# Storing two rows each of batches 10 and 11, instead of two rows of batch 11, so that one DMA engine is left out

## The chip, the cores and the metric

One NeuronCore of a Trainium2 chip runs the kernel. The metric is the device time of one execution in microseconds. Before the change it is 125.07 us, the median of 16 runs, which lie between 124.84 and 125.71 us.

## The reference

```python
batch, m, k, n = 16, 512, 512, 512
a: (batch, m, k) float32        b: (batch, n, k) float32
return np.matmul(a, b.transpose(0, 2, 1)).astype(np.float32)
```

That is sixteen products of 512x512 matrices. The second operand comes with k as its last axis, so both operands have to be transposed on the chip. The inputs are 2 x 16 MB, the output is 16 MB, and all of it passes through the core's 16 DMA engines.

## The kernel before, in words

**Tiling.** A batch of a matrix is 512 rows of 2 KB. A partition p of the 128 holds rows of one matrix that lie next to each other in memory. Loads take a pair of batches at once: 8 rows of 2 KB, one run of 16 KB a partition. Outputs are stored a batch at a time: partition p holds the rows 4p to 4p+3 (`J = 4`), so a whole row group is one run of 8 KB, two neighbouring rows are a run of 4 KB, and a single row is a run of 2 KB.

**Stages.** For each of 8 pairs VectorE casts the float32 inputs to bf16 (L154 to L167), TensorE transposes them (L223), ScalarE and VectorE copy the transposed tiles out of PSUM (L181, L168), TensorE multiplies (L242), and ScalarE copies the products from PSUM into `ob` (L201). `ob` has `NO = 7` slots, one a batch; the slot of batch n is n % 7. Each time that a batch is complete in `ob`, the semaphore `s_out` has reached n + 1.

**Queues.** Three engines issue DMAs, and each has a queue of its own on all 16 DMA engines. ScalarE issues 15 of the 16 loads (queue q10 of the page), SyncE (SP) issues one load and almost all stores (q1), and GpSimd (POOL) issues twelve small DMAs (q0). On one queue the DMAs move in the order of issue; a DMA engine takes turns between queues that have work for it. The order on SP is written out by hand in the loop L121 to L132: wait for `s_out`, store, next batch. Batch 15 is stored without its row 3 in that loop, and that last row of each partition is the kernel's last DMA (L263).

**ScalarE's waits on stores.** Before it fills the slot of batch n for n >= 7, ScalarE waits until the store of batch n - 7 has landed (L198). So it waits on the stores of batches 0 to 8 in the loop, and on those of batches 9 to 15, on `s_x` and on `s_y` at the end (L257 to L260).

**The store of batch 11.** All other batches are stored by one DMA over 128 partitions, 8 partitions to each of the 16 DMA engines. Batch `X = 11` is cut up. Its rows 1 and 2 go by one such DMA, as runs of 4 KB. Its rows 0 and 3 go by partition groups, as runs of 2 KB, and each group is written so that its partitions fall on chosen DMA engines:

- partitions 32 to 95 by one DMA of SP over 64 partitions (L129);
- partitions 0 to 15 by four DMAs of SP, each over the four partitions i, i+4, i+8, i+12 (L130, L131), and partitions 16 to 19 by one more of SP (L132), each over four partitions;
- partitions 20 to 31 and 96 to 127 by four rounds of POOL, each with a DMA over three partitions and one over eight (L117, L118). Ahead of these two, each round has a DMA of five partitions with 64-byte runs into a buffer `turn` that nothing reads (L114). 5 + 3 + 8 is 16: in each round the three DMAs take their DMA engines in turn.

POOL does this after it has passed all loads on to VectorE (L107, L108) and after `s_out` has reached 12 (L112). SP's seven DMAs of batch 11 follow its wait for the same value.

Of the kernel before, what the change touches and what calls it, by code (L numbers as in the profile page):

```python
# [10 lines left out]
def kernel(  # L11
# [6 lines left out]
    nc = tc.nc  # L18
    P = 128
    batch, M, K = a.shape  # L20
    _, N, _ = b.shape
    J = M // P
# [5 lines left out]
    bf16 = mybir.dt.bfloat16  # L28
    NL = 7
    NO = 7  # L30
    X = 11

    def sbuf(name, shape, dtype):
        return ctx.enter_context(nc.sbuf_tensor(name, shape, dtype))

    def sem(name):
        return tc.alloc_semaphore(name)

    with tc.tile_critical(no_gpsimd_drain=True):  # L41
# [8 lines left out]
        ob = sbuf("ob", [P, NO, J, N], f32)  # L50
# [20 lines left out]
        s_out = sem("s_out")  # L71
        s_x = sem("s_x")
        s_y = sem("s_y")
# [5 lines left out]
            out=ident[:], in_=ident[:], compare_op=mybir.AluOpType.not_equal, fill=1.0,  # L79
# [13 lines left out]
        def landed(n):  # L93
            return s_st[n % NO], 16 * (n // NO + 1)

        def store(n, lo=0, hi=J, step=1, part=slice(0, P), engine=nc.sync):
            rows = slice(lo, hi, step)
            return engine.dma_start(  # L98
                out[n].rearrange("(p j) n -> p j n", j=J)[part, rows], ob[part, n % NO, rows]
            )  # L100

        load(0, nc.scalar)
# [6 lines left out]

        nc.gpsimd.wait_ge(s_out, X + 1)  # L112
        for i in range(4):
            nc.gpsimd.dma_start(  # L114
                turn[:5, i], a[0, :5, :64].rearrange("p (x k) -> p x k", x=2)[:, :, :16]
            ).then_inc(s_y, 16)
            for part in (slice(20 + i, 32, 4), slice(96 + i, P, 4)):  # L117
                store(X, step=J - 1, part=part, engine=nc.gpsimd).then_inc(s_y, 16)  # L118

        nc.sync.wait_ge(s_ld[0], 32)  # L120
        for n in range(batch):  # L121
            nc.sync.wait_ge(s_out, n + 1)
            if n != X:
                store(n, hi=J if n < batch - 1 else J - 1).then_inc(landed(n)[0], 16)
                continue


            store(n, lo=1, hi=J - 1).then_inc(landed(n)[0], 16)
            store(n, step=J - 1, part=slice(32, 96)).then_inc(s_x, 16)  # L129
            for i in range(4):  # L130
                store(n, step=J - 1, part=slice(i, 16, 4)).then_inc(s_x, 16)  # L131
            store(n, step=J - 1, part=slice(16, 20)).then_inc(s_x, 16)  # L132

        def taker(engine):
            return lambda s, n: engine.wait_ge(s, n).then_inc(s, -n)  # L135
# [9 lines left out]
        with nc.Fori(0, pairs, engines=[dve]) as u:  # L145
            for x, (h, w, s_c, s_w) in enumerate(
# [4 lines left out]
                if x == 0:  # L151
# [4 lines left out]
                    out=h[:, J:, :], in_=src[:, J:, :HK]  # L156
                ).then_inc(s_c, 1)
                nc.vector.tensor_copy(out=w[:], in_=src[:, :, HK:]).then_inc(s_w, 1)  # L158
            for ko in range(KO):
# [5 lines left out]
                if ko == 1:  # L165
# [3 lines left out]
                    out=tb[:, ko, :],  # L169
# [7 lines left out]
        for u in range(pairs):  # L177
            for ko in range(KO):
                nc.scalar.wait_ge(s_ta, KO * u + ko + 1)
                for e in range(2):  # L180
                    c = nc.scalar.copy(  # L181
                        out=ta[:, ko, e * J * P:(e + 1) * J * P].rearrange(
                            "k (j p h) -> k j p h", j=J, h=2
                        ),
# [10 lines left out]
            for e in range(2):  # L195
                n = 2 * u + e
                if n >= NO:
                    nc.scalar.wait_ge(*landed(n - NO))  # L198
                for j in range(J):
                    nc.scalar.wait_ge(s_mm, J * n + j + 1)  # L200
                    c = nc.scalar.copy(  # L201
                        out=ob[:, n % NO, j, :].rearrange("m (p j) -> m p j", j=2 * J),
# [97 lines left out]
```

## Time and profile before

| what | value |
|---|---|
| median of 16 runs | 125.07 us (124.84 to 125.71) |
| the profiled execution | 124.7 us |
| its span, first to last instruction | 122.9 us |
| DMA traffic in the span | 50.35 MB, 410 GB/s |
| granted TensorE clock, mean | 0.98 |
| PE, DVE, ACT, POOL busy | 73%, 55%, 55%, 7% of the span |
| issue of the twelve DMAs of POOL | from 100.52 to 108.35 us |

The span leaves out 1.8 us of the profiled execution that lie around it. Times inside the span count from its first instruction. The page gives DMA as a mean over 16 engines; the trace behind it holds every packet with its queue, start, duration and size, but not the number of its engine.

### The profile page before, as it was taken

The numbers are of one execution on the slowest core, as the hardware profiler recorded it, in microseconds if no ns is written. First come the engines' busy times: TensorE is split into PE (matmuls) and PEld (weight loads), VectorE is DVE, ScalarE is ACT, GpSimd is POOL, SyncE is SP. The second block draws the span as 40 slices with busy tenths as digits, with TensorE's granted clock in tenths as the row PEclk, the third lists the DMA queues.
The fourth block names the chain that finished last, engine by engine and source line by source line (L and its number), as shares of the span: only waits on it lengthen the run. The fifth ranks groups of instructions, "written<-read, shape, count | busy, mean of one in ns | idle before, by whom it ended". The sixth has DMA issues, their size and how long they took to land. (4 is left out here: it accounts for less than half of the span.)

```text
span 122.9 us, 2255 instructions
## 1 busy us (share of the span) xinstructions
PE 90.1 (73%) x768; PEld 54.7 (45%) x768; DVE 67.9 (55%) x96; ACT 68.0 (55%) x130; POOL 8.5 (7%) x18
## 2 busy tenths in 40 slices
PE   0000089999999899989998999999799926997000
PEld 0000078347744764574477347644664415542000
DVE  0000598983895589389918983871987049500000
ACT  0400065468855966696589468765866076666000
POOL 2000000000000000000000000000000029920000
PEclk9999999999999999999999999999999999999965
DMA  4999999999999999999999999999999999999993
GB/s 139 411 427 427 437 427 427 432 432 427 427 427 427 427 368 408 440 413 427 427 429 427 429 440 413 451 427 419 435 424 429 424 419 427 428 401 425 429 413 125
DMA packets 5341, 50.35 MB, mean 410 GB/s; under 512 B 904, under 2 KB 904, under 8 KB 1500
## 3 DMA queue, kind: packets, MB, share of 16 engines
q10 hardware_dynamic: 2160, 31.46, 60.8%
q1 hardware_dynamic: 2796, 18.70, 36.2%
q0 software_dynamic: 384, 0.18, 0.5%
q14 instruction: 1, 0.01, 0.0%
HBM read 33.56 MB, written 16.78 MB: 410 GB/s over the span
## 5 line engine op out<-in xcount | busy, mean ns | idle before, releaser
L242 PE MATMUL ps<-tb,ta 128*128 128x512 bf16 x256 | 57.8, 379 | 0.4
L201 ACT COPY ob<-ps 128x512 f32<-128x512 f32 x64 | 34.3, 590 | 26.8 <-PE ps L242 22.1
L181 ACT COPY ta<-tp 128x512 bf16<-128x512 bf16 x64 | 33.0, 611 | 14.7 <-PE tp L223 14.2
L242 PEld LDWEIGHTS ps<-tb,ta 128*128 128x128 bf16 x256 | 24.1, 97 | 30.7 <-issue 4.0
L223 PE MATMUL tp<-ident,ha 128*128 128x128 bf16 x256 | 18.5, 224 | 18.5 <-PEq L135 18.0
L223 PEld LDWEIGHTS tp<-ident,ha 128*128 128x128 bf16 x256 | 15.8, 100 | 22.0 <-issue 20.3
L168 DVE COPY tb<-tp 128x1024 bf16<-128x1024 bf16 x32 | 21.3, 685 | 3.6 <-DVEq L135 3.6
L223 PE MATMUL tp<-ident,hb 128*128 128x128 bf16 x256 | 17.5, 223 | 3.7 <-PEq L135 3.5
L223 PEld LDWEIGHTS tp<-ident,hb 128*128 128x128 bf16 x256 | 15.3, 100 | 4.9 <-issue 4.7
L154 DVE CAST ha<-ld 128x1024 bf16 x8 | 5.5, 691 | 14.4 <-POOLq L108 13.6
L163 DVE COPY ha<-wa 128x2048 bf16<-128x2048 bf16 x8 | 5.5, 691 | 12.5 <-DVEq L135 12.5
L154 DVE CAST hb<-ld 128x1024 bf16 x8 | 5.5, 690 | 8.2 <-DVEq L135 8.1
L158 DVE CAST wa<-ld 128x2048 bf16 x8 | 9.8, 1221 | 0.0
L158 DVE CAST wb<-ld 128x2048 bf16 x8 | 9.8, 1220 | 0.0
L114 POOL DMA_DIRECT2D turn<-in_a_dram x4 | 2.7, 665 | 98.8 <-DMA ld<-in_b_dram 98.8
L155 DVE CAST hb<-ld 128x1024 bf16 x8 | 5.5, 686 | 0.0
L155 DVE CAST ha<-ld 128x1024 bf16 x8 | 5.5, 686 | 0.0
L167 DVE COPY hb<-wb 128x2048 bf16<-128x2048 bf16 x8 | 5.5, 684 | 0.0
L98 POOL DMA_DIRECT2D out_dram<-ob x8 | 5.2, 651 | 0.0
L176 ACT ACT_TABLE_LOAD x1 | 1.3, 1283 | 4.0 <-issue 4.0
L78 POOL TENSOR_SCALAR_AFFINE_SELECT ident<-ident 128x128 bf16<-128x128 bf16 x1 | 0.3, 289 | 0.2 <-POOL ident L76 0.2
L76 POOL MEMSET ident<- 128x128 bf16 x1 | 0.2, 205 | 0.5 <-SPq L41 0.5
(5 smaller groups left out, 0.6 us busy)
## 6 DMA issues: line engine op xcount, KB each, us to landing
ld<-in_a_dram ACTq DMA_DIRECT2D x8, 2048.0 KB, 29.2
ld<-in_b_dram ACTq DMA_DIRECT2D x7, 2048.0 KB, 26.9
out_dram<-ob SPq DMA_DIRECT2D x14, 1024.0 KB, 28.8
ld<-in_b_dram SPq DMA_DIRECT2D x1, 2048.0 KB, 12.3
out_dram<-ob SPq DMA_DIRECT2D x1, 768.0 KB, 7.6
out_dram<-ob SPq DMA_DIRECT2D x1, 512.0 KB, 24.6
out_dram<-ob SPq DMA_DIRECT2D x2, 256.0 KB, 7.5
out_dram<-ob POOLq DMA_DIRECT2D x4, 32.0 KB, 6.0
```

Source lines behind the costliest of these rows:

```text
L98: return engine.dma_start(out[n].rearrange("(p j) n -> p j n", j=J)[part, rows], ob[part, n % NO, rows])
L114: nc.gpsimd.dma_start(turn[:5, i], a[0, :5, :64].rearrange("p (x k) -> p x k", x=2)[:, :, :16]).then_inc(s_y, 16)
L154: nc.vector.tensor_copy(out=h[:, :J, :], in_=src[:, :J, :HK])
L155: nc.vector.tensor_copy(out=h[:, J:, :], in_=src[:, J:, :HK]).then_inc(s_c, 1)
L158: nc.vector.tensor_copy(out=w[:], in_=src[:, :, HK:]).then_inc(s_w, 1)
L163: nc.vector.tensor_copy(out=ha[:], in_=wa[:]).then_inc(s_ca, 1)
L167: nc.vector.tensor_copy(out=hb[:], in_=wb[:]).then_inc(s_cb, 1)
L168: nc.vector.tensor_copy(out=tb[:, ko, :], in_=tp[:, 2 + ko % 2].rearrange("k j p -> k (j p)"),).then_inc(s_eb, 1)
L181: c = nc.scalar.copy(out=ta[:, ko, e * J * P:(e + 1) * J * P].rearrange("k (j p h) -> k j p h", j=J, h=2), in_=tp[:, ko % 2, :, e * HP:(e ...
L201: c = nc.scalar.copy(out=ob[:, n % NO, j, :].rearrange("m (p j) -> m p j", j=2 * J), in_=ps[:, j, :].rearrange("m (j p) -> m p j", j=2 * J),)
L223: t = nc.tensor.transpose(tp[:, 2 * x + g, j, :], h[:, j, g * P:(g + 1) * P], ident[:])
L242: t = nc.tensor.matmul(ps[:, j, :], ta[:, ko, (e * J + j) * P:(e * J + j + 1) * P], tb[:, ko, :].rearrange("k (j p) -> k j p", j=2 * J)[:, ...
```

## The change

Batch 11's rows 0 and 3 are no longer the rows that are stored by groups. Now rows 0 and 1 of batch 10 and rows 0 and 1 of batch 11 are, both batches in the same DMAs. `X` becomes 10. The stores of batches 10 and 11 over 128 partitions take rows 2 and 3 only. The groups of partitions, the engines that issue them, their number and `turn` are the same; each partition now sends two runs of 4 KB (one of each batch) where it sent two runs of 2 KB. The value of `s_out` that POOL waits for stays 12. SP issues the six grouped DMAs after batch 11's own store.

```diff
-    X = 11
+    X = 10
+    H = J // 2
...
-        def store(n, lo=0, hi=J, step=1, part=slice(0, P), engine=nc.sync):
-            rows = slice(lo, hi, step)
+        def store(n, lo=0, hi=J):
+            return nc.sync.dma_start(
+                out[n].rearrange("(p j) n -> p j n", j=J)[:, lo:hi], ob[:, n % NO, lo:hi]
+            )
+
+        def store_two(part, engine):
+
             return engine.dma_start(
-                out[n].rearrange("(p j) n -> p j n", j=J)[part, rows], ob[part, n % NO, rows]
+                out[X:X + 2].rearrange("e (p j) n -> p e j n", j=J)[part, :, :H],
+                ob[part, X % NO:X % NO + 2, :H],
             )
...
-        nc.gpsimd.wait_ge(s_out, X + 1)
+        nc.gpsimd.wait_ge(s_out, X + 2)
         for i in range(4):
             nc.gpsimd.dma_start(
                 turn[:5, i], a[0, :5, :64].rearrange("p (x k) -> p x k", x=2)[:, :, :16]
             ).then_inc(s_y, 16)
             for part in (slice(20 + i, 32, 4), slice(96 + i, P, 4)):
-                store(X, step=J - 1, part=part, engine=nc.gpsimd).then_inc(s_y, 16)
+                store_two(part, nc.gpsimd).then_inc(s_y, 16)
...
             nc.sync.wait_ge(s_out, n + 1)
-            if n != X:
-                store(n, hi=J if n < batch - 1 else J - 1).then_inc(landed(n)[0], 16)
-                continue
-
-
-            store(n, lo=1, hi=J - 1).then_inc(landed(n)[0], 16)
-            store(n, step=J - 1, part=slice(32, 96)).then_inc(s_x, 16)
-            for i in range(4):
-                store(n, step=J - 1, part=slice(i, 16, 4)).then_inc(s_x, 16)
-            store(n, step=J - 1, part=slice(16, 20)).then_inc(s_x, 16)
+            store(n, H if n in (X, X + 1) else 0, J if n < batch - 1 else J - 1).then_inc(
+                landed(n)[0], 16
+            )
+            if n == X + 1:
+
+
+                for part in (slice(32, 96), *(slice(i, 16, 4) for i in range(4)), slice(16, 20)):
+                    store_two(part, nc.sync).then_inc(s_x, 16)
```

## The prediction

> **What bounds the kernel now.** I read the page's slices first, then the queues, the chain, the waits of the last 24 us, and then single packets.
>
> ```profile
> PE   0000089999999899989998999999799926997000
> DMA  4999999999999999999999999999999999999993
> GB/s 139 411 427 427 437 427 427 432 432 427 427 427 427 427 368 408 440 413 427 427 429 427 429 440 413 451 427 419 435 424 429 424 419 427 428 401 425 429 413 125
> ```
>
> From the second slice to the last but one the DMA engines are full, at about 427 GB/s. The last three slices have no TensorE work, only DMA.
>
> ```profile
> PE 6%; ACT 1%; issue 0%
> ```
>
> The chain explains only 7% of the span: it breaks off at a DMA.
>
> ```profile
> POOL turn L114 <- DMA ld<-in_b_dram: 98.8, 1, 98.8
> ACT ob L201 <- DMA out_dram<-ob: 3.5, 1, 3.5
> ```
>
> Of the waits after 99 us these two end with DMAs: the engines wait for transfers, not transfers for engines. So the time is the work of the slowest of 16 DMA engines.
>
> ```profile
> q10 hardware_dynamic: 2160, 31.46, 60.8%
> q1 hardware_dynamic: 2796, 18.70, 36.2%
> q0 software_dynamic: 384, 0.18, 0.5%
> ```
>
> The mean over 16 engines hides which one that is, so I threaded the trace's packets. On one DMA engine a packet starts 3 to 4 ns before the recorded end of the one before it, and each engine must take each queue's packets in the order of issue. Under these two rules all packets from 1.97 us on fall into 16 chains. A chain's group shows in the pieces of batch 11: four chains move the ten extra 2 KB pieces of L131 and L132 (engines 0 to 3), eleven move four 4096-byte packets of q0 (engines 5 to 15), and one has neither: the spared engine, 4. Each chain ends with the completion of the kernel's last store (L263):
>
> ```
> group    end of the chain, us
> 4        121.326
> 0 to 3   120.724  120.953  121.100  121.140
> 5 to 15  121.065  120.953  120.927 ... 120.554 (eleven)
> ```
>
> Engine 4 is last although it carries 16 KB less, ahead of the next by 0.186 us. The reason is in its packets. An 8 KB packet takes 309 ns, 1727 of 1792 times. Summed over what each size normally takes, engine 4's packets lost 0.46 us between 73.5 and 101.2 us, 0.87 us between 101.2 and 115, and 0.01 us after; no other engine lost more than 0.13 us after 73.5. The large part begins when POOL issues its first DMA (100.52) and ends soon after q0's last packet (114.16).
>
> **The change, part by part.** Starts follow each other by the recorded duration less 3.5 ns: 306 ns for 8 KB (309), 155.5 for 4 KB (159), 80 for 2 KB (84). For the packets of batches 10 and 11 alone:
>
> Engine 4, before: 8 x 306 (batch 10) + 8 x 155.5 (rows 1, 2) + 8 x 80 (its share of L129) = 4332 ns. After: 8 x 155.5 for each half store and 8 x 155.5 for its share of partitions 32 to 95 = 24 x 155.5 = 3732. That is **-0.600 us**.
>
> Engines 0 to 3, before: 4332 + 10 x 80 = 5132. After: 3732 + 10 x 155.5 = 5287. **+0.155 us** each: they carry what engine 4 gives up.
>
> Engines 5 to 15, before: 4332 + 4 x 155.5 (q0 packets of 4096) = 4954. After: 3732 + 4 x 306 = 4956 if q0 moves 8 KB packets, 4976 if 4 KB ones. No trace shows q0 with 4 KB runs, so I keep both: 0.00 to +0.02 us.
>
> The longer runs earn nothing in themselves: 512 pieces before (128 of 8 KB, 128 of 4 KB, 256 of 2 KB) and 512 of 4 KB after, with the same bytes.
>
> New ends: engine 4 at 121.326 - 0.600 = 120.73; the slowest of 0 to 3 at 121.140 + 0.155 = 121.295; the slowest of the rest at 121.065 + 0.02 = 121.085. The last end moves from 121.326 to 121.295, **-0.03 us**. What follows the last packet (SP is released at 121.83, the span ends at 122.9) stays.
>
> What I cost at nothing, with its cover:
> - Rows 0 and 1 of batch 10 are issued after batch 11's store, so their place in q1 is one half store later. The whole store of batch 10 was issued at 84.92 us, but q1 reached it only when batch 9's store was through, at about 105.8: 20.9 us of backlog. Without it each us of delay would leave the DMA engines idle for one. ScalarE's waits in the loop are on batches 0 to 8, all ahead of it in q1.
> - SP issues seven DMAs at batch 11 as before. They were through at 95.39 us, though the last two issues took 1.8 and 3.6 us, and the next store was issued at 99.54. So a longer stall of up to 4.1 us there would cost nothing; past that it would delay the store of batch 12, which moved only from about 111 us.
> - POOL's twelve DMAs. Page part 6 and the same view for 100 us on give them as
>
> ```profile
> out_dram<-ob POOLq DMA_DIRECT2D x4, 32.0 KB, 6.0
> turn<-in_a_dram POOLq DMA_DIRECT2D x4, 0.6 KB, 5.8
> out_dram<-ob POOLq DMA_DIRECT2D x4, 12.0 KB, 6.2
> ```
>
> with KB each and us from issue to landing. POOL waits for the same value of `s_out`, 12. It is held by the last load until 100.52 anyway, and then issues DMAs of the same shape. Nothing is queued behind them but the end. With twice the bytes q0 may end some us after 114.16; the final wait is passed at 121.83, so there are 7 us of cover. If twelve DMAs spread longer, that alone costs nothing.
>
> The Trainium skill (DMA: Bandwidth & Descriptors, section Latency and other measured facts) says that DMA engines 7 and 15 are usually the slow ones, with a guess that the descriptor rings of GpSimd's DMAs crowd a port. By that rule engine 4 would be the wrong one to relieve, and the change would only put 0.155 us on engines 0 to 3. The packets above differ on which: the losses are on the one spared engine, and two others with such losses do not exist here; they agree that the losses come with GpSimd's DMAs. I go by the packets.
>
> **The base.** The profiled execution took 124.7 us, 0.37 below the median. -0.03 us on it is 124.67, and the same step from the median of 125.07 gives 125.04.
>
> **The rivals.**
>
> *Engine 4's lead is larger in the timed runs (faster).* The gain is the lead less 0.155, at most 0.600. The profiled execution shows a lead of 0.186, but it was quicker than all 16 runs. If the 0.37 us to the median are all engine 4's losses, the lead is 0.56 and the gain 0.40: 124.67. For it: engine 4's losses (1.34 us after 73.5) are the one irregular item late in the profile. Against: between 40 and 50 us all sixteen engines lose 0.3 to 0.7 us in common stalls, and variation of these, or of the 1.8 us outside the span, moves all ends alike. The full 0.600 would give 124.47.
>
> *GpSimd's larger DMAs slow engine 4 in proportion (slower).* 0.87 us of losses coincide with q0. If they go with q0's bytes, which double for the eight stores, engine 4 loses 0.87 more and gains 0.60: +0.27, or 125.34. It decides once the losses grow by more than 0.57 (0.60 less the 0.03), two thirds. For it: the coincidence in time. Against: q0 carries only 0.18 MB, its DMAs and runs stay the same in number, and the losses begin at about 101 us, when q0's first packet moved only at 105.30: they belong to issuing or fetching, not to the bytes. The lower bound is that they shrink with engine 4's fewer packets, worth nothing since engine 4 is then not last.
>
> *The bytes do not land where they should.* Whether POOL's 3- and 8-partition DMAs keep to engines 5 to 15 with 4 KB runs, and the four-partition DMAs of SP to engines 0 to 3, no trace shows. The patterns keep their shape (partitions, two runs, contiguous), which speaks for it. If engine 4 kept its share and some other got 16 KB too much, that is 4 x 155.5 = 0.62 us on an engine that ended at 121.1: 121.7, +0.4 us.
>
> *Engines 0 to 3 are last already.* Then the change costs +0.155, or 125.22. That is inside what counts as no change.
>
> **How the numbers follow.** About 0.2% (0.25 us) is what a measurement of this kernel can tell from no change. Engines 0 to 3 take over as last, with a lead of engine 4 up to 0.4 us or none: 0.47, own range 124.82 to 125.22. Larger lead: 0.32, from 124.47 to 124.82. Losses in proportion to bytes: 0.11, at 125.34. Misplaced bytes: 0.10, most of it slower, at 125.45. Faster 0.32, same 0.48, slower 0.20. The range leaves out the best part of the large leads and the worst of the misplaced: 124.60 to 125.40.
>
> **What would show it.** Threaded again, the chain without extra pieces should end near 120.7, one of the four with ten extra pieces last, near 121.3, and the eleven unchanged. The table of queues should show q0 with about twice the bytes, and the DMA issues of POOL with 64 and 24 KB. Engine 4's losses between 101 and 115 us should stay near 0.9 us. I am wrong if engine 4 is still last, if losses appear on another engine, or if a slice before the last drops below the 427 GB/s level because q1 ran dry.

## The result and the profile after

The changed kernel takes 125.50 us, the median of 8 runs (125.44 to 125.66), against 125.07 us, the median of 44 runs of the kernel before (124.76 to 125.71). The ratio is 1.0034, with a 95% interval of 1.0020 to 1.0047: slower by 0.43 us. The profiled execution took 125.47 us with a span of 123.7.

The slices of the page after, DMA share and rate:

```profile
DMA  4999999999999999999999999999999999999991
GB/s 127 403 429 429 429 429 424 424 429 429 429 435 429 435 387 421 429 416 443 403 429 443 429 421 429 427 429 429 432 432 432 413 424 421 413 407 402 428 407 57
```

The engines are as full as before by the share, but the rate falls to 407 and 402 GB/s in the neighbouring slices 36 and 37, where before only the first of the two (401) was that low. A digit of 9 hides this: the share counts the time that packets take, also of those that take longer than their size needs. First the rows of the table of queues for the whole span, then POOL's issues (KB each, us from issue to landing):

```profile
q1 hardware_dynamic: 2796, 18.52, 35.9%
q0 software_dynamic: 512, 0.36, 0.9%
```

```profile
out_dram<-ob POOLq DMA_DIRECT2D x4, 64.0 KB, 6.6
out_dram<-ob POOLq DMA_DIRECT2D x4, 24.0 KB, 6.5
turn<-in_a_dram POOLq DMA_DIRECT2D x4, 0.6 KB, 6.1
```

q0 carries twice its bytes, as the edit says, and its DMAs land 0.3 to 0.6 us later after their issue. The waits after 99 us are the same two, and the chain breaks off at a DMA as before:

```profile
POOL turn L121 <- DMA ld<-in_b_dram: 98.9, 1, 98.9
ACT ob L206 <- DMA out_dram<-ob: 3.6, 1, 3.6
```

```profile
PE 8%; ACT 1%; issue 0%
```

So neither engines nor issue explain the time. One view shows where it went: the stretch from 109 to 113 us (columns: us, busy time and count of PE, PEld, DVE, ACT, POOL, granted clock, DMA share, GB/s). The kernel before, then the changed one:

```profile
109.00:113.00 4.00, 3.79 (x18) 1.52 (x16) 0.00 (x0) 2.70 (x6) 0.00 (x0) 1.00 1.04 417
```

```profile
109.00:113.00 4.00, 4.00 (x20) 1.81 (x19) 0.00 (x0) 2.56 (x5) 0.00 (x0) 1.00 1.03 396
```

The share is nearly the same (1.04 and 1.03), and the rate falls from 417 to 396 GB/s. These are the 4 us in which SP's small DMAs move. The packets, threaded into engines as for the prediction, show which of them lost the time. "Lost" is always a packet's duration less what its size normally takes:

```
the last small DMA of SP (partitions 16 to 19), engines 0 to 3, two packets each:
           start us, ns           start us, ns        end of the chain, us
before     110.65  84             110.73   84         120.72
(2 KB)     110.88  84             110.96   84         120.95
           110.89  84             110.97  215         121.10
           111.08  84             111.16   84         121.14
after      110.64 159             110.80  533         121.27
(4 KB)     110.74 159             110.90 1245         122.07
           111.09 261             111.38  808         122.11
           110.71 396             111.19 1112         122.23
```

All other packets of the small DMAs take 159 ns. In this one DMA the four engines lose 3.4 us in sum. Without these losses they would have ended by 121.36; with them all four end after the other twelve, three of them about 1 us later. Engine 4 ended at 121.07, the other eleven at 120.48 to 121.07 (before: 120.55 to 121.07). The packets bear no engine numbers: 0 to 3, 4 and 5 to 15 are names for the chains by the pieces that they carry.

### The profile page after: what moved, and what is told of

The parts are those of the page before. It is cut to its first block, busy times and chain, and to the rows that moved or that the text cites. A ratio compares the mean times of both kernels' runs of the same rounds, so it can differ in the third digit from the quotient of the medians.

```text
span 123.7 us, 2255 instructions
## 1 busy us (share of the span) xinstructions
PE 92.0 (74%) x768; PEld 57.1 (46%) x768; DVE 68.0 (55%) x96; ACT 67.9 (55%) x130; POOL 8.5 (7%) x18
## 5 line engine op out<-in xcount | busy, mean ns | idle before, releaser
L228 PE MATMUL tp<-ident,ha 128*128 128x128 bf16 x256 | 20.3, 235 | 18.2 <-PEq L140 17.8
L228 PEld LDWEIGHTS tp<-ident,ha 128*128 128x128 bf16 x256 | 17.3, 106 | 21.9 <-issue 20.1
L228 PE MATMUL tp<-ident,hb 128*128 128x128 bf16 x256 | 18.5, 229 | 3.3 <-PEq L140 3.3
L228 PEld LDWEIGHTS tp<-ident,hb 128*128 128x128 bf16 x256 | 16.4, 103 | 3.9 <-issue 3.6
```

Of the source, the lines that this page charges most:

```text
L228: t = nc.tensor.transpose(tp[:, 2 * x + g, j, :], h[:, j, g * P:(g + 1) * P], ident[:])
```

## The experiments

Theory A is that four engines that read (or write) neighbouring partitions (or rows) at the same moment hold each other up. Its rivals are: B, a chance stall of one execution; C, that any four-partition DMA with 4 KB runs into two batches stalls; D, that partitions 16 to 19 themselves are the limit, whoever reads them; and the bytes of POOL's DMAs, for the losses of engine 4. In the texts on record the "fifth" and "sixth" small DMA count from the one over partitions 32 to 95; below, the five after it are numbered 1 to 5.

**The changed kernel again.** No edit.

> The changed kernel once more, on one chip with the next three. Theory A (the last DMA of a group, partitions 16 to 19 on engines 0 to 3 at once, stalls when its pieces are 4 KB long because all four engines read neighbouring partitions or write neighbouring rows at the same time): the stall is there again in this profile, 2 to 4 us of lost packet time in sum on the four chains between 110 and 113 us, and the time is 0.2 to 0.5% above the kernel before. Rival B (a chance stall of one execution, and the slower time comes from something else): the stall is not there or elsewhere, with the time as slow.

125.57 us against 125.11 on the same chip, ratio 1.0037 (1.0024 to 1.0050). The same DMA, and no other, lost 3.3 us in sum; its second packets took 631, 760, 907 and 1236 ns. So it is no chance of one execution.

**Steps of five.**

```diff
-                for part in (slice(32, 96), *(slice(i, 16, 4) for i in range(4)), slice(16, 20)):
+                for part in (slice(32, 96), *(slice(i, 20, 5) for i in range(5))):
```

> Same as the changed kernel, but the twenty partitions 0 to 19 go by five DMAs over the partitions i, i+5, i+10, i+15 instead of four over i, i+4, i+8, i+12 and one over 16 to 19. Bytes, runs and number of pieces of each engine stay the same; no DMA has two partitions of one group of four. Theory A: the lost packet time of engines 0 to 3 between 110 and 113 us falls from 3.4 us in sum to under 0.5, their ends from 122.23 us to about 121.2, and the time falls by about 1.0 us to 124.5, below the kernel before (125.07). Rival C (any four-partition DMA with runs of 4 KB into two batches stalls engines 0 to 3): no change, about 125.5. Rival D (the port of partitions 16 to 19 itself is the limit, whoever reads it): losses stay but spread over the five DMAs, time between.

124.79 us (12 runs, 124.66 to 124.99), 0.9973 of the kernel before (0.9960 to 0.9986), and 0.78 us under the changed kernel on the same chip. Of the 40 packets of the five small DMAs 38 take 159 ns; the two of one engine in DMA 5 (4, 9, 14, 19) take 313 and 419: 0.41 us lost instead of 3.3. The four chains ended at 121.04, 121.06, 121.25 and 121.43, the last with the 0.41 us in it. The time falls by 0.78 us and not by the expected 1.0: engine 4 itself ended at 121.33 here, so mending the four chains alone could have brought 0.1 us more at most. The same stretch of this version:

```profile
109.00:113.00 4.00, 4.00 (x21) 1.77 (x19) 0.00 (x0) 2.69 (x6) 0.02 (x1) 1.00 1.04 421
```

The rate is back at 421 GB/s. With the same bytes, runs and engines, the grouping alone makes the difference. Rival C falls; rival D too, in the form that any reading of 16 to 19 costs the same.

**No sparing.** `store_two`, its DMAs on SP and on POOL, `turn`'s DMAs and the waits for them are removed. The line of the stores (the rest is left out here):

```diff
-            store(n, H if n in (X, X + 1) else 0, J if n < batch - 1 else J - 1).then_inc(
+            store(n, 0, J if n < batch - 1 else J - 1).then_inc(
```

> No sparing at all: batches 10 and 11 are stored like the others, and POOL issues no DMA. If engine 4's losses (0.87 us between 101 and 115 us) come from POOL's DMAs, they vanish: engine 4 ends with the others near 121.1 us and the time is 124.8 to 125.1. If they come from something else, engine 4 keeps them and carries 16 KB more than in the kernel before: its end is at 121.33 + 0.60 = 121.93 and the time about 125.7.

125.23 us, ratio 1.0013 (1.0000 to 1.0025): between the two times expected. One chain is last by 0.65 us, at 121.76. No extra pieces mark an engine here, but this chain has losses like those of engine 4: 0.50 us between 73.5 and 101.2 us and 0.62 between 101.2 and 115, and no other chain has any after 73.5. No DMA of POOL exists here:

```profile
DMA packets 4753, 50.34 MB, mean 408 GB/s; under 512 B 528, under 2 KB 528, under 8 KB 784
## 3 DMA queue, kind: packets, MB, share of 16 engines
q10 hardware_dynamic: 2160, 31.46, 60.4%
q1 hardware_dynamic: 2592, 18.88, 36.3%
```

(no row of q0). So POOL's DMAs are not the main cause of engine 4's losses. The threaded profiles with them show 0.74 to 0.87 us in that stretch, so 0.12 to 0.25 us may be theirs.

**Reading or writing.** The changed kernel with the rows of two DMAs exchanged in the output:

```diff
-                for part in (slice(32, 96), *(slice(i, 16, 4) for i in range(4)), slice(16, 20)):
+                for part in (slice(32, 96), *(slice(i, 16, 4) for i in range(3))):
                     store_two(part, nc.sync).then_inc(s_x, 16)
+                store_two(slice(16, 20), nc.sync, slice(3, 16, 4)).then_inc(s_x, 16)
+                store_two(slice(3, 16, 4), nc.sync, slice(16, 20)).then_inc(s_x, 16)
```

(the last argument is where the rows are written; these are DMAs 4 and 5).

> The changed kernel with the targets of two DMAs exchanged (the output has these rows exchanged): the fifth small DMA of SP reads partitions 16 to 19 but writes the rows of partitions 3, 7, 11, 15; the sixth reads partitions 3, 7, 11, 15 and writes the rows of 16 to 19. If the reading of four neighbouring partitions stalls, packets over 159 ns stand in the fifth, and the sixth is clean; if the writing of neighbouring rows stalls, it is the sixth alone. 2 to 4 us of losses in sum are expected in the one and under 0.3 us in the other.

DMA 4, which reads 16 to 19 and writes rows far apart, lost 2.4 us in sum (296 to 922 ns for the second packets, 478 for one of the first). DMA 5, which reads 3, 7, 11, 15 and writes the neighbouring rows, lost nothing: eight packets of 159 ns. So it is the reading side, by one run. Its time was 125.58.

**Five blocks of neighbours.**

```diff
+                for part in (slice(32, 96), *(slice(i, i + 4) for i in range(0, 20, 4))):
```

> Same as the changed kernel, but partitions 0 to 19 go by five DMAs of SP over 0-3, 4-7, 8-11, 12-15 and 16-19, each on engines 0 to 3 at once. If reading any four neighbouring partitions by four engines stalls, all five stall: 3 to 4 us of losses in sum in each, 15 to 18 us in all, the ends of engines 0 to 3 near 125 us and the time near 128. If it is peculiar to partitions 16 to 19, only the last stalls and the time is 125.5.

Neither came true. Blocks 0-3, 4-7 and 8-11 lost nothing, although all four engines were in the first of them at once; 12-15 lost 0.79 us in sum and 16-19 0.92. The one run took 125.67.

**Two engines at a time.** (The final wait on `s_x` counts one DMA more.)

```diff
-                ... slice(16, 20)):
+                ... slice(16, 20, 2), slice(17, 20, 2)):
```

> Same as the changed kernel, but partitions 16 to 19 go by two DMAs over two partitions each, 16 and 18, then 17 and 19. They fall on two engines, so only two read the group of four partitions at once, and these two carry 8 KB more than before and the other two 8 KB less. If the stall is the four engines' sharing of what one port gives, two engines lose much less: under 1 us in sum instead of 3.4. If any sharing stalls, 2 us or more. The time is 125.0 to 125.4 in the first case, the two chains ending 0.3 us later than in the version with steps of five.

The loss lies between the two: 1.09 us in sum, in four packets of 278 to 595 ns. The one run took 125.61, slower than expected for the first case. Threaded, two chains have twelve pieces each and two have eight, so each of the two DMAs has two readers, and all four long packets are on the two chains. Two readers lose time, a third of what four lose. But the last of the four, 384 ns from 112.07 on, began when the other chain's last piece had ended (111.74): its engine read partitions of this group with no other of engines 0 to 3 beside it.

**The kernel before in steps of five.**

```diff
-            for i in range(4):
-                store(n, step=J - 1, part=slice(i, 16, 4)).then_inc(s_x, 16)
-            store(n, step=J - 1, part=slice(16, 20)).then_inc(s_x, 16)
+            for i in range(5):
+                store(n, step=J - 1, part=slice(i, 20, 5)).then_inc(s_x, 16)
```

> The kernel before (two rows of batch 11 alone, runs of 2 KB) with partitions 0 to 19 grouped in steps of five. In the profile before the DMA over 16 to 19 lost only 0.13 us, on a chain that was not last, so the grouping has nothing to mend: 125.0 to 125.1, no difference within 0.2%. If the grouping by itself brings the gain of 0.3% that it brought with the change, 124.8.

125.04 us against 125.06, ratio 0.9994 (0.9981 to 1.0008). The grouping brings nothing where there is no stall to mend. In this profile engine 4 ended at 122.00 and the next chain at 121.23: a lead of 0.77 us, with the bytes of the kernel before.

**Steps of five, last first.** The changed kernel in steps of five, with `for i in reversed(range(5))`.

> The version with steps of five, its five DMAs in reverse order, so that partitions 4, 9, 14, 19 come first and 0, 5, 10, 15 last. In the version with steps of five one chain still lost 0.41 us in its last DMA (4, 9, 14, 19), and that chain was last. If the loss belongs to these partitions it moves to the first small DMA; if it belongs to the moment (other engines starting on the next store), it stays in the last. Time 124.7 to 124.85 either way, below the kernel before.

124.75 us, ratio 0.9971 (0.9959 to 0.9984). Two packets lost 0.43 us in sum, by the threading (less certain in this profile than in the others) both in DMA 4 (1, 6, 11, 16). So in these two profiles the loss that is left belongs neither to one group nor to the last place. The changed kernel in steps of five takes less time than both the kernel before and the changed kernel in either order, 0.27 and 0.29% under the kernel before; the two orders cannot be told apart.

**Partitions 16 to 19 first.**

```diff
+                for part in (slice(32, 96), slice(16, 20), *(slice(i, 16, 4) for i in range(4))):
```

> Same as the changed kernel, but the DMA over partitions 16 to 19 comes first of SP's five small ones, about 1.3 us earlier (near 109.4 us instead of 110.7). If these partitions read by four engines at once stall at any moment, the first small DMA loses 2 to 4 us in sum and the time stays at 125.5. If the stall needs the moment (the other engines being in the next whole store, which they enter between 109.7 and 110.9 us), the losses fall under 1 us and the time is 124.7 to 124.9, as with steps of five.

125.48 us, ratio 1.0020 (1.0005 to 1.0034; the kernel before had 125.29 on this chip). The DMA over 16 to 19, now at 109.4 us, lost 2.9 us in sum (780, 1202 and 1306 ns for three second packets), the four after it nothing. So the stall goes with these partitions, and it does not need the next whole store.

**The blocks in reverse.** `range(16, -4, -4)` in the kernel of five blocks.

> The five blocks of four neighbouring partitions in reverse order: 16-19, 12-15, 8-11, 4-7, 0-3. In the forward order the first three blocks (0 to 11) lost nothing, the fourth (12-15) 0.8 us and the fifth (16-19) 0.9 us in sum. If it goes by partitions, the first two lose now, 0.8 us or more each, and 0-3 at the end nothing. If it goes by the moment, 16-19 and 12-15 are clean and the losses are in 4-7 and 0-3.

Neither came true in full: 16-19 lost 1.80 us in sum, 12-15 nothing, 8-11 1.39, 4-7 nothing, 0-3 0.80. The one run took 125.92. So the stall is not peculiar to 16-19: other blocks of neighbours have it too, in some orders. After the first two stalls the four chains entered the next DMA spread over 0.6 and 1.0 us, and it lost nothing. The spread alone does not explain it: in the second case three of the four entered within 0.16 us.

## Why the prediction was wrong

**The step that failed** is "Engines 0 to 3 ... +0.155 us each": it put the cost of reading the longer pieces at nothing beyond their size. The bytes were right: in the changed kernel 34 of the 40 pieces take 159 ns, and without the stall (steps of five) the chain that was the last of the four before ended at 121.25. It is known by a packet of queue q14 near 49 us (8 KB, 309 to 345 ns), and it ended at 121.14 and 121.23 in the two profiles with the old bytes. That is +0.02 to +0.11 for +0.155, within the scatter. What the term left out is that the last DMA lost 0.37 to 1.19 us on each of the four chains, so that the last of them ended at 122.23 instead of 121.295. The prediction had named losses on another engine as a sign of being wrong. And I had looked at the packet that hints at the stall: 215 instead of 84 ns, in that DMA in the profile before. I counted it among the 0.13 us that another engine lost, and did not ask what it becomes when the pieces are longer. Before, a chain passed through that DMA in 0.17 us, and the four entered it at 110.65, 110.88, 110.89 and 111.08: at most two were in it at once, and the one packet that lost was on one of such a pair. After, it takes 0.32 us, and three entered within 0.10 us. Whether the length of the pieces or this closeness made the difference no run separates. "The longer runs earn nothing in themselves" stands; that they cost nothing does not.

**The new last chain** is one of the four with extra pieces, as forecast, but that was luck: the stall put it there, not the bytes. In steps of five, the three of these chains that lost nothing ended at 121.04 to 121.25, before engine 4 at 121.33.

**Engine 4's -0.600 us** holds within the scatter. In the seven cleanly threaded profiles that spare it 32 KB it ended at 120.72 to 121.47, mean 121.13; in the two with 16 KB at 121.33 and 122.00, mean 121.66. That is -0.53, from two profiles on one side.

**The first rival, a larger lead of engine 4,** was sound as a mechanism and shows once the stall is gone: the steps of five bring -0.32 us (125.11 to 124.79), where the rival said up to -0.40. The profiled execution of the kernel before (124.7) was quicker than all of its 44 runs, and its lead of 0.186 was small: the other profile with these bytes shows 0.77. I should have given this case more weight, and my base from one profile less.

**The second rival, losses with q0's bytes,** named the wrong cause for the right sign. Between 101.2 and 115 us engine 4 lost 0.76 us with the doubled bytes, 0.87 before and 0.62 with no q0 at all. That the losses come with POOL's DMAs, in which I agreed with the Trainium skill (DMA: Bandwidth & Descriptors, Latency and other measured facts), falls with the same numbers as the main cause. Which number the slow engine has in the skill's count the packets do not show; they show that it is the chain that the kernel leaves out.

**The other two rivals** did not come true. The bytes landed where they should: eleven chains with 32 KB of q0 each, four with ten extra pieces, one with neither. And engines 0 to 3 were not last already: both profiles with the old bytes have engine 4 last, by 0.19 and 0.77 us.

**The other terms costed at nothing** stayed so. SP's last small DMA was issued by 95.38 us (before 95.39), ahead of the next store at 99.55; q0 ended at 116.05, well before SP's final release at 122.6; and no slice of the loop runs dry.

**What stays open.** It is shown that the loss comes with reading partitions 16 to 19 by several engines in one DMA (steps of five, exchanged rows, two at a time, 16 to 19 first): the six profiles in which four engines read them in 4 KB pieces all have it, with 0.92 to 3.4 us. What more it needs is not shown. Other blocks of neighbours were read by four engines with a loss in some places and without one in others, which speaks against a simple limit on a port that neighbours share. Nor do engines 0 to 3 always need each other for it: with two at a time the last long packet came after the other engine's last piece, and in five blocks too (411 ns from 112.06 on; the other long chain had ended its piece at 111.92). In both versions with steps of five one engine of the four lost alone, each time in a DMA that has one of the partitions 16 to 19 (19, then 16). So a weaker form of rival D, that these partitions are special in themselves, is not excluded. Why engine 4 is slow from about 74 us until compute ends is not settled either: all the threaded profiles show it, with and without POOL's DMAs.

## What to carry to other kernels

When a kernel is bound by DMA, the mean over the 16 engines hides the bound: thread the packets into engines and compare their ends before moving bytes. When bytes are moved to chosen engines, ask also which partitions these engines read at the same moment: groups with a step that gives every engine another neighbourhood are as easy to write, and here turned a loss of 0.34% into a gain of 0.27%. A single packet that takes longer than its size, off the critical path, is a sign of a limit that the change may hit in earnest.

## What the runs showed of the hardware

- Four engines that read partitions 16 to 19 at once, two 4 KB pieces each, needed up to 1306 ns for a packet that otherwise takes 159. The same pieces over partitions five apart: 159, apart from two packets of one engine in each profile, of up to 467.
- The page's DMA share does not show it: 1.03 with the stall and 1.04 without, at 396 and 421 GB/s. The rate does.
- One engine of the 16, the spared one (without sparing, the one that ends last), loses 0.45 to 0.53 us between 73.5 and 101.2 us and 0.62 to 0.87 us between 101.2 and 115 in the ten cleanly threaded profiles, and at most 0.14 us after.
